# Writing the first five pairs of row gathers into the final stage of a hybrid decoder layer, the adding gather ahead of the plain one

## The chip, the cores and the metric

One core of a Trainium2 chip runs the whole kernel. The time is device microseconds of an execution. Five engines work beside each other: TensorE (PE, with its weight loads as PEld), VectorE (DVE), ScalarE (ACT), GpSimd (POOL) and SyncE (SP), and 16 DMA engines move data. Each engine takes its own instructions in order and waits for the others at semaphores. SP issues most plain transfers; POOL issues the indirect ones, and writes their descriptors itself.

## The reference, cut to what matters

The layer is a token mixer (attention and a gated delta rule), a layer norm, a mixture of experts and a last layer norm. The change touches the last two:

```python
h = layer_norm(DEEPNORM_ALPHA * h + mix, ln1_g[i], ln1_b[i])
ffn = hierarchical_moe(h.reshape(b * l, D_MODEL), ...)
h = layer_norm(DEEPNORM_ALPHA * h + ffn, ln2_g[i], ln2_b[i])
return h[:, N_META:]
```

In `hierarchical_moe` each of the 1024 tokens goes to one group of 4 and there to two experts of 8, so that of 32 experts two add a weighted row of 1024 numbers to the token. A token's last row is the layer norm of its own row plus these two expert rows.

## The kernel before, in words

The last phase (`phase4`) goes over the 32 experts in order. For each, POOL gathers the rows of up to 128 tokens from HBM (`gather`, line 1503), TensorE computes the expert, and POOL stores its 128 result rows to the HBM tensor `ysd` (`keep`, line 1576). Experts 30 and 31 are not stored: their rows stay in SBUF, and TensorE spreads them over the tokens with one-hot matrices `oh`. The loop over the experts runs under `manual_schedule`, in which every engine's instructions keep the order of the source; it ends with `self.man.close()` at line 1671.

For each of the eight token tiles t (128 tokens each) the final stage needs two gathers from `ysd`, made by `combine` (line 1579), 128 rows of 4 KB each:

- the **plain gather** writes one expert row per token into `ybs[t]`. These tiles lie in memory that held weights, so their names in the profile are `wo4l`, `wo6h`, `wo6l` and `wo4h`, two token tiles in each.
- the **adding gather** adds the other expert row, in the DMA engines, to `yts[t]` (`yt` in the profile), which holds the token's own row already.

`rows(t)` issues both. For t = 0 to 4 (`GE = 5`) it is called in `phase4` after `overflow`; for t = 5 to 7 it is called from the final stage.

`overflow` is a branch on a count `nov` that each engine loads and compares (lines 1693 and 1695). Its body handles tokens that an expert has no room for; here the count is zero and the body is jumped over, but the path around it is a block of its own, in which each engine waits at semaphores before it goes on. The adding gathers must come after the branch, because its body may add to `yts` too. The plain gathers need not, and outside `manual_schedule` a scheduler chooses the order.

`finish` is the final stage, again under `manual_schedule`. For a tile t, `total` lets TensorE sum the rows of experts 30 and 31 (line 1782: four matmuls in `part(t, 0)`, four in `part(t, 2)`) and the plain gather's tile through an identity matrix (line 1793) into PSUM; VectorE adds the sum to `yt` (line 1794). Then come `square` (ACT), `rstd` (DVE and POOL, lines 101 and 102), `shift` (DVE, line 1806), `scale` (ACT, line 120), `gain` (DVE, line 1812), `store` (DVE, line 1815, and the output's DMA from SP). `TO` gives each step a due time and the steps of all tiles are written out sorted by t + due time. `shift(t)` calls `more(t + GE)` first, so the pairs of gathers for tiles 5, 6 and 7 stand on POOL behind `rstd` of tiles 1, 2 and 3, and these stand behind `total` of tiles 2, 3 and 4 on VectorE.

Of the kernel before, what the change touches and what calls it, by code (L numbers as in the profile page):

```python
# [12 lines left out]
ALU = mybir.AluOpType  # L13
# [4 lines left out]
P = 128  # L18
# [9 lines left out]
NE = 32  # L28
# [19 lines left out]
GE = 5  # L48
# [33 lines left out]
class Trunk:  # L82
# [1394 lines left out]
    def phase4(self):  # L1477
# [100 lines left out]
        def combine(src, fi, n, t, k, o, **kw):  # L1578
            nc.gpsimd.indirect_dma_start(out=o, out_offset=None, in_=src,  # L1579
                                         in_offset=bass.IndirectOffsetOnAxis(ap=fi[:, t, k:k + 1], axis=0),  # L1580
                                         bounds_check=n - 1, oob_is_err=False, **kw)

        def rows(t):
            combine(self.ysd, fi, (NE - 2) * P + 1, t, 1, ybs[t])
            combine(self.ysd, fi, (NE - 2) * P, t, 0, yts[t], compute_op=ALU.add)

        def over(fi):
            for k in range(2):
# [19 lines left out]
        fi = self.small.tile([P, NT, 2], I32, name="fi", bufs=1)  # L1608
# [12 lines left out]
        for e in range(NE):  # L1621
            more = e + 1 < NE
# [23 lines left out]
            if e == FE:  # L1646
                self.rb.close()
                fp = fin.enter_context(self.pool("fin", "left"))
                yts = [fp.tile([P, D], F32, name=f"yt{t}") for t in range(NT)]
# [29 lines left out]
                                         in_=y, in_offset=None, bounds_check=16 * P - 1, oob_is_err=False)  # L1679

        self.overflow(item, ps, fp.tile([P, D], F32, name="xo"), over)
        for t in range(GE):
            rows(t)
        pss.close()
        sq = mp.tile([P, KT, P], F32R, name="xh", bufs=1).rearrange("p a b -> p (a b)")
        self.finish(fp, g2, b2, yts, oh, ys, sq, ybs, lambda t: t < NT and rows(t))
        fin.close()
        es.close()
# [81 lines left out]
    def finish(self, fp, g2, b2, yts, oh, ys, sq, ybs, more):  # L1770
        nc, tc = self.nc, self.tc
        st = [fp.tile([P, 4], F32, name=f"st{t}") for t in range(NT)]
        rs = [fp.tile([P, 2], F32, name=f"rs{t}") for t in range(NT)]
        with self.psum("psf") as ps, tc.manual_schedule():
            pfs = {}

            def part(t, j0):
                if j0 == 0:
                    pfs[t] = ps.tile([P, D], F32, name="pf", bufs=4)
                for c in range(2):  # L1780
                    for j in (j0, j0 + 1):
                        nc.tensor.matmul(pfs[t][:, c * 512:(c + 1) * 512], oh[j // 2][:, t],
                                         ys[j // 2][j % 2][:, c * 512:(c + 1) * 512], start=(j == 0), stop=False)

            part(0, 0)
            part(1, 0)
            def total(t):
                if t > 1:
                    part(t, 0)
                part(t, 2)  # L1790
                for c in range(2):
                    ns = slice(c * 512, (c + 1) * 512)
                    nc.tensor.matmul(pfs[t][:, ns], self.ident, ybs[t][:, ns], start=False, stop=True)
                nc.vector.scalar_tensor_tensor(yts[t], pfs.pop(t), 1.0, yts[t], op0=ALU.mult, op1=ALU.add,  # L1794
                                               accum_out=st[t][:, 0:1])

            def square(t):
                nc.scalar.activation(st[t][:, 1:2], st[t][:, 0:1], AF.Copy, scale=-1.0 / D)
                nc.scalar.activation(sq, yts[t], AF.Square, bias=st[t][:, 1:2], accum_out=st[t][:, 2:3])

            def rstd(t):
                self.rsqrt_into(rs[t][:, 0:1], st[t][:, 2:3], 1.0 / D, LN_EPS / ALPHA ** 2)

            def shift(t):
                more(t + GE)
                nc.vector.tensor_tensor(rs[t][:, 1:2], st[t][:, 1:2], rs[t][:, 0:1], op=ALU.mult)  # L1806

            def scale(t):
                self.ln_apply(yts[t], P, rs[t], yts[t])

            def gain(t):
                nc.vector.tensor_tensor(yts[t], yts[t], g2, op=ALU.mult)  # L1812

            def store(t):
                (nc.vector if t in TV else nc.gpsimd).tensor_tensor(yts[t], yts[t], b2, op=ALU.add)  # L1815
                nc.sync.dma_start(self.out[0, t * P:(t + 1) * P, :], yts[t])

            ops = (total, square, rstd, shift, scale, gain, store)
            for _, i, t in sorted((t + TO[i], i, t) for t in range(NT) for i in range(len(ops))):
                ops[i](t)  # L1820
# [59 lines left out]
```

## Time and profile before

| | us |
|---|---|
| median of 3 runs | 1189.67 (1184.7 to 1194.07) |
| profiled execution, its own time | 1192.47 |
| its span | 1190.7 |
| its mean granted TensorE clock | 0.953 |
| busy over the span: PE, DVE, ACT, POOL | 92%, 73%, 53%, 24% |

Starts are microseconds from the span's start. The change acts on the last 70 us alone: the end of the expert loop (to about 1126), the branch, and the final stage. The shares over the whole span say nothing on these, so the profile has to be read there by its timeline, its waits and its stretches.

### The profile page before, as it was taken

The page shows a single profiled execution, that of the slowest core. Times are in us where ns is not written, and L with a number is a line of the kernel's source. Part 1 is how long each engine was busy: PE and PEld are TensorE (multiplying, and loading weights), DVE is VectorE, ACT ScalarE, POOL GpSimd, SP SyncE. Part 2 cuts the span into 40 slices and gives each one's busy share as a digit, 9 for nine tenths or more (in the row PEclk, how much of TensorE's full clock was granted, in tenths as well). Part 3 has the DMA queues.
Part 4 walks back from the last instruction along what each step waited for, and adds up shares of the span by engine and source line. Part 5 has one row for each costly group of instructions (what it writes and reads, how often), then busy time and mean ns, then how long its engine had stood idle before and what let it go on. Part 6 is the DMA issues. An engine that isn't in the chain of part 4 may idle for free. (4 is left out here: it accounts for less than half of the span.)

```text
span 1190.7 us, 19809 instructions
## 1 busy us (share of the span) xinstructions
PE 1094.4 (92%) x7061; PEld 935.6 (79%) x7061; DVE 863.4 (73%) x1672; ACT 630.9 (53%) x1310; POOL 289.7 (24%) x389
## 2 busy tenths in 40 slices
PE   6999999999989979899989999857999999999973
PEld 4999999999989968777776777755777777777741
DVE  7941357988433238989847687786999999999827
ACT  3443346855223236566536464234777777777633
POOL 3523102412000013444324331001111111112253
PEclk9999999999999978999979999776999999999987
DMA  7411134466695577976547561756999999599676
GB/s 287 178 63 45 37 108 126 139 175 220 212 241 196 184 254 222 253 238 192 179 133 203 171 233 64 317 194 224 375 406 396 396 406 399 200 377 416 263 166 214
DMA packets 112441, 271.01 MB, mean 228 GB/s; under 512 B 31075, under 2 KB 60523, under 8 KB 99540
## 3 DMA queue, kind: packets, MB, share of 16 engines
q1 hardware_dynamic: 100816, 236.43, 57.6%
q0 software_dynamic: 11232, 32.22, 8.6%
q8 instruction: 57, 0.93, 0.3%
q10 hardware_dynamic: 292, 1.07, 0.2%
q14 instruction: 44, 0.36, 0.1%
HBM read 213.83 MB, written 64.53 MB: 234 GB/s over the span
## 5 line engine op out<-in xcount | busy, mean ns | idle before, releaser
L186 PE MATMUL pj<-hTh,wfh 128*128 128x346 f32 (+1 forms) x480 | 156.1, 325 | 0.1
L187 PE MATMUL pj<-hTl,wfh 128*128 128x346 f32 (+1 forms) x480 | 155.8, 325 | 0.0
L188 PE MATMUL pj<-hTh,wfl 128*128 128x346 f32 (+1 forms) x480 | 155.7, 324 | 0.0
L881 DVE TENSOR_TENSOR_SCAN mm<-mm,zero 128x272 f32<-128x272 f32 (+3 forms) x64 | 89.4, 1411 | 19.8 <-ACT mm L868 17.6
L186 PEld LDWEIGHTS pj<-hTh,wfh 128*128 128x128 f32 x480 | 90.8, 189 | 0.5 <-issue 0.3
L188 PEld LDWEIGHTS pj<-hTh,wfl 128*128 128x128 f32 x480 | 90.9, 189 | 0.1
L187 PEld LDWEIGHTS pj<-hTl,wfh 128*128 128x128 f32 x480 | 90.8, 189 | 0.2
L1535 PE MATMUL ph<-w13h,xh 128*128 128x512 f32 x192 | 88.6, 461 | 0.0
L179 PE MATMUL pj<-wvh,hTl 128*128 128x256 f32 (+3 forms) x280 | 78.9, 285 | 3.6 <-DVE hTl L97 3.5
L178 PE MATMUL pj<-wvl,hTh 128*128 128x256 f32 (+3 forms) x280 | 78.9, 284 | 2.2 <-DVE wvl L97 2.2
L177 PE MATMUL pj<-wvh,hTh 128*128 128x256 f32 (+3 forms) x280 | 79.5, 288 | 0.2 <-ACT hTh L96 0.2
L1465 DVE TENSOR_TENSOR w13l<-raw,w13h 128x512 fp32r<-128x512 f32 x126 | 77.9, 685 | 0.0
L1503 POOL DMA_INDIRECT xg<-h1d,ix x32 | 34.1, 1064 | 171.3 <-PE tp L1513 136.6
L1537 PE MATMUL ph<-w13h,xl 128*128 128x512 f32 x192 | 75.3, 392 | 0.0
L1536 PE MATMUL ph<-w13l,xh 128*128 128x512 f32 x192 | 74.9, 390 | 0.0
L1464 ACT ACTIVATE w13h<-raw 128x512 fp32r<-128x512 f32 x126 | 68.0, 621 | 0.0
L872 POOL TENSOR_SCALAR_AFFINE_SELECT mm<-mm 128x128 f32<-128x128 f32 x64 | 39.8, 627 | 111.9 <-ACT mm L868 111.5
L868 ACT ACTIVATE mm<-z 128x512 f32<-128x512 f32 (+1 forms) x80 | 44.3, 564 | 38.4 <-PE z L866 29.1
L866 PE MATMUL z<-qk 128*128 128x416 f32 (+6 forms) x224 | 59.8, 374 | 4.8 <-ACT kuw L778 2.9
L1465 DVE TENSOR_TENSOR w2l<-raw,w2h 128x512 fp32r<-128x512 f32 x96 | 59.9, 686 | 2.2 <-ACT w2h L1464 0.2
L96 ACT ACTIVATE xh<-tp 128x512 fp32r<-128x512 f32 x64 | 31.4, 491 | 50.1 <-DVE xf L1522 43.2
L902 ACT ACTIVATE wt<-tp 128x512 f32<-128x512 f32 (+1 forms) x80 | 41.6, 556 | 28.4 <-PE tp L901 27.7
(441 smaller groups left out, 2977.9 us busy)
## 6 DMA issues: line engine op xcount, KB each, us to landing
raw<-in_w SPq DMA_DIRECT2D x67, 1024.0 KB, 12.3
ysd<-y POOLq DMA_DIRECT2D x30, 512.0 KB, 8.5
qk<-qkd SPq DMA_DIRECT2D x16, 520.0 KB, 5.5
ht<-hscr SPq DMA_DIRECT2D x16, 512.0 KB, 3.4
wo4h<-in_w SPq DMA_DIRECT2D x8, 1024.0 KB, 13.4
wo4l<-in_w SPq DMA_DIRECT2D x7, 1024.0 KB, 14.0
wo6l<-in_w SPq DMA_DIRECT2D x7, 1024.0 KB, 12.1
wo6h<-in_w SPq DMA_DIRECT2D x7, 1024.0 KB, 11.4
```

What stands on the lines that cost most here:

```text
L177: nc.tensor.matmul(o[:p, :n], xh, wh[:, kt, ws], start=(kt == 0), stop=False)
L178: nc.tensor.matmul(o[:p, :n], xh, wl[:, kt, ws], start=False, stop=False)
L179: nc.tensor.matmul(o[:p, :n], xl, wh[:, kt, ws], start=False, stop=(kt == KT - 1))
L186: nc.tensor.matmul(o[:, :n], wh[:, kt], self.hTh[:, kt, c0:c0 + n], start=(kt == 0), stop=False)
L187: nc.tensor.matmul(o[:, :n], wh[:, kt], self.hTl[:, kt, c0:c0 + n], start=False, stop=False)
L188: nc.tensor.matmul(o[:, :n], wl[:, kt], self.hTh[:, kt, c0:c0 + n], start=False, stop=(kt == KT - 1))
L881: nc.vector.tensor_tensor_scan(mm[:, c0:c1][:, ::-1], mm[:, c0:c1][:, ::-1], self.zero1.to_broadcast([P, c1 - c0]), 1.0, op0=ALU.mult, op1 ...
L1464: nc.scalar.activation(wh, raw, AF.Copy)
L1465: (nc.gpsimd if k in pool else nc.vector).tensor_tensor(wl, raw, wh.bitcast(F32), op=ALU.subtract)
L1535: nc.tensor.matmul(ph, xh[:, kt], wh, start=False, stop=False)
L1536: nc.tensor.matmul(ph, xh[:, kt], wl, start=False, stop=False)
L1537: nc.tensor.matmul(ph, xl[:, kt], wh, start=False, stop=(kt == ks[-1]))
```

## The change

`rows(t)` issues the adding gather first and the plain one second; the loop that called it for t = 0 to 4 in `phase4` goes; and `finish` calls it for these five tiles as its first step, inside `manual_schedule`.

```diff
         def rows(t):
+            combine(self.ysd, fi, (NE - 2) * P, t, 0, yts[t], compute_op=ALU.add)
             combine(self.ysd, fi, (NE - 2) * P + 1, t, 1, ybs[t])
-            combine(self.ysd, fi, (NE - 2) * P, t, 0, yts[t], compute_op=ALU.add)
@@ phase4
         self.overflow(item, ps, fp.tile([P, D], F32, name="xo"), over)
-        for t in range(GE):
-            rows(t)
         pss.close()
@@ finish
         with self.psum("psf") as ps, tc.manual_schedule():
             pfs = {}
+            for t in range(GE):
+                more(t)
```

On POOL, at the end of the expert loop, the order before was this (`ysd<-y` are the expert stores, `wo..<-ysd` the plain gathers, and line 1695 is the branch over the overflow body):

```order
L1576 DMA ysd<-y 128x1024 x4
L1579 DMA wo4l<-ysd,fi 128x1024 x2
L1579 DMA wo6h<-ysd,fi 128x1024 x2
L1579 DMA wo6l<-ysd,fi 128x1024
L1693 TENSOR_LOAD nov
L1695 COMPARE_AND_BRANCH
```

The scheduler had put the five plain gathers ahead of the branch. In the changed kernel the branch follows the stores directly (its lines count two less):

```order
L1576 DMA ysd<-y 128x1024 x4
L1691 TENSOR_LOAD nov
L1693 COMPARE_AND_BRANCH
L1695 IOTA n_12659 128x16
```

The five plain gathers are gone from this place. The second place is POOL behind the branch's join, where the difference between the two kernels is this (`yt_` is the tile of an adding gather, and 11839 to 11843 are the token tiles 0 to 4):

```order
 L1579 DMA yt_11839<-ysd,fi 128x1024
+L1579 DMA wo4l<-ysd,fi 128x1024
 L1579 DMA yt_11840<-ysd,fi 128x1024
+L1579 DMA wo4l<-ysd,fi 128x1024
 L1579 DMA yt_11841<-ysd,fi 128x1024
+L1579 DMA wo6h<-ysd,fi 128x1024
 L1579 DMA yt_11842<-ysd,fi 128x1024
+L1579 DMA wo6h<-ysd,fi 128x1024
 L1579 DMA yt_11843<-ysd,fi 128x1024
```

The fifth plain gather (`wo6l`) follows right behind. Ten gathers now stand here where five stood, and each plain gather follows its tile's adding one. The third place is the wait of POOL on the path around the overflow body, which stands in both kernels with the same list (DMASW are the completion semaphores of the transfers that POOL issued):

```order
L1695 ISA [waits Pool_49,DMASW4_49,DMASW5_49,DMASW3_49,DMASW6_49,DMASW2_49,DMASW7_49,DMASW1_49,DMASW0_49]
```

It names every lane of POOL's transfers. What was issued on them last, ahead of it, is five plain gathers before and the expert stores now.

## Rows read from the trace of the kernel before

**Rows 1.** Chain of work that ended last, four of its pieces: start, us, what.

```profile
1128.27 10.39 DMA wo6h<-ysd,fi
1138.66 0.11 POOLq L1695
...
1173.53 1.23 DVE yt L1794 x2
...
1185.53 1.23 DVE yt L1815
```

**Rows 2.** Waits from 1118 us to the end: total us, times, longest.

```profile
DVE yt L1794 <- DMA yt<-ysd,fi: 25.3, 8, 13.8
```

**Rows 3.** Single lines 1695, 1579, 1576 (from 1090 us), 1503; durations ns min/median/max.

```profile
L1695 POOLq EVENT_SEMAPHORE  x5: 17/43/8036, 1125.7 to 1138.3; - x5
...
L1579 POOLq EVENT_SEMAPHORE  x15: 17/43/2768, 1118.5 to 1161.2; - x15
...
DMA to landing us min/median/max: 2.9/8.2/9.0
...
L1503 POOL DMA_INDIRECT xg<-h1d,ix x32: 986/1071/1316, 810.2 to 1085.7; - x32
```

**Rows 4.** Timeline of POOL: start, us, instruction, idle before it and its releaser.

```profile
1118.48 0.53 POOL L1576 DMA_DIRECT2D ysd<-y  x1 [9.13 <-ACT w2h L1464]
1122.46 4.17 POOL L1579 DMA_INDIRECT wo4l<-ysd,fi  x1 [3.45 <-issue]
...
1130.88 1.00 POOL L1579 DMA_INDIRECT wo6l<-ysd,fi  x1 [0.31 <-issue]
1139.73 1.61 POOL L1579 DMA_INDIRECT yt<-ysd,fi  x1 [7.86 <-issue]
...
1159.74 2.12 POOL L1579 DMA_INDIRECT yt<-ysd,fi  x1 [0.30 <-issue]
...
1162.65 1.05 POOL L1579 DMA_INDIRECT wo4h<-ysd,fi  x1 [0.18 <-issue]
```

**Rows 5.** Stretches: length, busy per engine, clock, DMA share (last but one), GB/s.

```profile
1121.00:1127.00 6.00, 5.30 (x24) 3.95 (x22) 5.45 (x9) 1.51 (x4) 4.23 (x2) 1.00 0.00 1
1127.40:1137.00 9.60, 7.33 (x24) 5.52 (x25) 3.34 (x5) 2.59 (x5) 3.56 (x4) 0.82 0.81 271
1137.00:1142.00 5.00, 5.00 (x16) 2.77 (x16) 0.00 (x0) 0.00 (x0) 1.97 (x2) 1.00 0.01 3
1142.00:1158.10 16.10, 12.15 (x43) 7.60 (x41) 5.28 (x14) 6.35 (x12) 10.19 (x9) 0.95 0.95 176
1158.10:1173.50 15.40, 11.42 (x28) 5.81 (x28) 10.89 (x18) 9.32 (x15) 9.49 (x8) 0.83 0.95 238
```

**Rows 6.** Timeline of DVE, the same columns.

```profile
1123.34 2.35 DVE L1637 TENSOR_TENSOR xg<-slots,ixt 128x1024 fp32r<-128x1024 f32 x2
...
1145.88 1.23 DVE L1794 SCALAR_TENSOR_TENSOR yt<-pf,yt 128x1024 f32<-128x1024 f32 x1 [13.81 <-DMA yt<-ysd,fi]
...
1158.08 1.23 DVE L1794 SCALAR_TENSOR_TENSOR yt<-pf,yt 128x1024 f32<-128x1024 f32 x1 [0.80 <-DMA yt<-ysd,fi]
...
1159.23 1.22 DVE L1812 TENSOR_TENSOR yt<-yt,g 128x1024 f32<-128x1024 f32 x1
...
1160.50 1.22 DVE L1815 TENSOR_TENSOR yt<-yt,b 128x1024 f32<-128x1024 f32 x1
1163.85 1.23 DVE L1794 SCALAR_TENSOR_TENSOR yt<-pf,yt 128x1024 f32<-128x1024 f32 x1 [2.14 <-DMA yt<-ysd,fi]
...
1169.10 1.23 DVE L1794 SCALAR_TENSOR_TENSOR yt<-pf,yt 128x1024 f32<-128x1024 f32 x1 [1.61 <-DMA yt<-ysd,fi]
```

**Rows 7.** Timeline of PE: the plain gather's tile through the identity matrix.

```profile
1137.05 1.88 PE L1793 MATMUL pf<-wo4l,ident 128*128 128x512 f32 x4
...
1150.44 1.88 PE L1793 MATMUL pf<-wo6l,ident 128*128 128x512 f32 x4
...
1159.43 3.78 PE L1793 MATMUL pf<-wo6l,ident 128*128 128x512 f32 x4 [5.28 <-DMA wo6l<-ysd,fi]
```

## The prediction

> **What bounds the kernel now.** I read the chain that ended last first, since only its end can move. Its last long piece is VectorE's adding of a tile's sum to `yt` for tile 7 at 1173.53; behind it stands VectorE work without a gap to 1186.76 and the last store to 1190.7 [rows 1]. So total(7), as I call that instruction, sets the end, and the 17.2 us behind it follow whenever it comes. Next I read the waits of this stage: VectorE waits for adding gathers 25.3 us in eight waits, the longest 13.8 us, which is the wait of total(0), at 1145.88 [rows 2, 6]. The final stage is therefore fed by POOL's gathers.
>
> Why does the first adding gather come so late? The chain answers: a plain gather landed at 1138.66, and only then POOL's queue left line 1695, the branch [rows 1]. The rows of that line show one wait of 8.0 us on POOL's queue [rows 3]. On the path around the overflow body POOL waits for all its transfers, and the last of these were the five plain gathers, issued from 1122.46 to 1131.88 [rows 4]. The stretches show the price: the DMA engines are idle from 1137 to 1142 (share 0.01), between the plain gathers (0.81) and the adding ones (0.95) [rows 5]. From 1142 they are nearly always busy, so that gap is most of what can be won.
>
> **The change, part by part.** Nothing is added or taken away: 16 gathers before, 16 after. Five plain ones move from ahead of the branch to behind it, each behind its adding one.
>
> *The join.* POOL's last transfer ahead of the branch is now the store at 1118.48 [rows 4]. It landed within 2.9 us (the shortest store; POOL's queue then waited at most 2.77 us for it ahead of the first gather) [rows 3]: 1121.4. From the landing at 1138.66 to the first adding gather at 1139.73 were 1.07 us [rows 1, 4]. So the first adding gather starts at 1122.5, not at 1139.73.
>
> *Its descriptors.* The gather that began at 1122.46 took 4.17 us, where the next ones took 1.00 [rows 4]. VectorE was then in operations with two SBUF inputs until 1125.69 [rows 6]; the gather ended 0.94 us behind that, about one gather's own time. The adding gather takes this place, and it needs 1.61 in place of 1.00 [rows 4]: I take 4.17 + 0.6 and end it at 1127.3. The bound from the other side is the 32 gathers of the expert loop at 1071 ns in the median, 1316 at most [rows 3], which means no block: then it ends at 1124.1, 3.2 us earlier. I take the blocked value, because that row has the same neighbours at the same time.
>
> *The DMA time.* The engines began to move data 0.7 us behind the end of the first adding gather (1141.34 to 1142.0) [rows 4, 5], so they begin at 1128.0 now, 14.0 us earlier. What they must move has grown, though: the plain gathers are in the same queue. A plain one costs 9.6 us x 0.81 / 5 = 1.55 us [rows 5]. An adding one costs (1158.08 - 1145.88) / 4 = 3.05 us [rows 6]; the first was added 3.9 us behind the start of the transfers, so a landing takes some 0.8 more. A pair is 4.6 us. Pairs 0 to 4: 1128.0 + 23.0 = 1151.0, landed at 1151.8. POOL writes a pair's descriptors in about 3.2 us (1.00 + 1.61 and two gaps of 0.3) [rows 4], less than 4.6, so the queue stays fed.
>
> *What is late next.* The plain tile now lands last, and behind it TensorE must take it through the identity matrix, 1.88 us [rows 7]. Before, this lay beside the wait for the adding gather (1137.05 against 1145.88); that cover is gone. TensorE reached tile 4's at 1150.44 [rows 7], so it now waits some 1.4 us there; for tiles 0 to 2 TensorE itself is the limit. total(4) comes at 1151.8 + 1.9 = 1153.7, before at 1158.08 [rows 6].
>
> *Pairs 5 to 7.* They stay behind rstd of tiles 1 to 3 on POOL, and so behind total(2) to total(4). The first gather of pair 7 followed total(4) by 4.57 us (1162.65 from 1158.08) [rows 4, 6]; now at 1158.3, with its descriptors 2.12 us (the dearest adding one) [rows 4] and 0.7 to the transfers: 1161.1. Pairs with one output store beside them cost 5.25 and 4.43 us, by total(5) to total(7) at 1163.85, 1169.10 and 1173.53 [rows 1, 6], on average 4.84. Pairs 5 and 6 end at 1151.0 + 9.7 = 1160.7; pair 7 starts at 1161.1 and ends at 1165.9. With 0.8 for landing and 1.9 for TensorE, total(7) comes at 1168.6 in place of 1173.53: **4.9 us earlier**.
>
> *The skill's rule.* The Trainium skill ("SBUF — State Buffer", section "SBUF: two separate sides") says that VectorE and GpSimd share a port pair under an exclusive lock, so that GpSimd cannot write descriptors until such a VectorE operation ends. The row at 1122.46 agrees with that. The row at 1159.74 does so only in part: VectorE's lines 1812 and 1815 covered it until 1161.72, yet it ended at 1161.86 after 2.12 us [rows 4, 6]; a full lock would have left its 1.6 us to be done behind 1161.72. By the full lock, the adding gather of pair 7 could be pushed behind two such operations (2 x 1.22 us), and the gain would be 4.9 - 2.4 = 2.5 us.
>
> *Bounds of the pair's price.* With 4.43 for all eight, transfers end at 1163.4 and the gain is 7.4; with 5.25 they end at 1170.0 and it is 0.8. No row shows adding and plain gathers alternate without stores.
>
> Sum: the span goes from 1190.7 to 1185.8, the profiled execution from 1192.47 to 1187.6. That execution lies 2.8 us above the median of the runs; against the median of 1189.67 the forecast is **1184.8 us**.
>
> **The rivals.**
> - *The branch still holds POOL* (slower). If something else than the plain gathers keeps POOL at the join to 1138, all eight pairs start at 1142.0 and total(7) comes at 1168.6 + 14.0 = 1182.6, 9.1 us later: 1198.8. It decides from a first adding gather later than 1127.4, where the 4.9 us are used up. For it: the wait names every lane, also POOL's own. Against it: the chain has a plain gather's landing right ahead of its end [rows 1], and the store needs 2.9 us only [rows 3]. Chance 0.07.
> - *No block on the first gather.* Transfers begin at 1124.8, gain 8.1, time 1181.6. For it: the 32 gathers at 1071 ns, many beside a busy VectorE. Against it: the 4.17 us row. Chance 0.2.
> - *Alternating gathers cost more*, 5.25 us a pair, and TensorE, waiting between tiles, falls to its lower clock, at which the identity takes 3.78 us as at 1159.43 [rows 7]: -0.8 + 1.9 = 1.1 us slower, 1190.8; with one of the two, 1186.7 to 1188.9. For it: TensorE's 5.28 us wait there was followed by that clock. Against it: the expected waits are about 1.2 us a tile (4.6 less 3.35 of matmuls, a quarter of the way from 1137.05 to 1150.44) [rows 7]. Chance 0.18.
> - *The late gathers wait for VectorE.* The adding gather of pair 7 begins behind both operations of lines 1812 and 1815, 2.4 us later: gain 2.5, 1187.2. For it: it stands beside them, as the one at 1159.74 did. Against it: that one took 2.12 us only [rows 4]. Chance 0.05.
>
> **How the numbers follow.** The forecast (gain 3 to 6.5) has 0.5. The predicted time is its 1184.8, for which the range takes in the gain without the block (1181.6) less 3 us, and the dear pairs with the lower clock (1190.8) plus 2: three runs of the kernel before spread over 9.4 us, and their median can be off by some 3. That is 1178.5 to 1193. Left out are the first rival and a gain beyond 11 us. About 1%, 11.9 us, is what a measurement of this kernel can tell from no change. Faster than that needs the unblocked gather and cheap pairs together (8.1 + 2.5 = 10.6) and more: 0.05. Slower needs the first rival with dear pairs (9.1 + up to 4.1): 0.04. Within 1%: 0.91.
>
> **What would show it.** Right: the wait of 8.0 us on line 1695's POOL queue shrinks to under 3; the first `yt` gather starts near 1122.5 and takes over 4 us; the idle 5 us of the DMA engines are gone; total(0) comes near 1139, total(4) near 1153.7, total(7) near 1168.6; the identity of tiles 3 to 7 waits for `wo` gathers; 17.2 us remain behind total(7). Wrong: a first `yt` gather behind 1127.4; pairs beyond 5.3 us; the identity of the late tiles at 3.8 us; or DMA idle between pairs 6 and 7.

## The result, and the profile after

The changed kernel takes 1184.26 us in the median of 20 runs (1180.01 to 1191.7), the kernel before 1190.36 in 20 (1184.37 to 1194.38). The ratio is 0.995 (95% interval 0.9933 to 0.9967), which is 4 to 8 us less. The forecast was 1184.8. In a later comparison beside other experiments the same kernel gave 0.9964 (0.9928 to 0.9999).

The profiled execution of the changed kernel has a span of 1178.9 us, 11.8 less than that of before. That is not the gain. POOL's last expert store begins at 1118.48 in the one and at 1111.55 in the other, so 6.9 us of it lie ahead of the first instruction that the change moves, where both kernels do the same. From here on I count from that store, in each trace. Behind it the span is 72.2 us before and 67.4 now, **4.9 us** less, and the forecast was 4.9.

POOL's timeline of the changed kernel answers to [rows 4] (start, us, instruction, idle before it):

```profile
1111.55 0.53 POOL L1576 DMA_DIRECT2D ysd<-y  x1 [9.13 <-ACT w2h L1464]
1116.84 3.46 POOL L1579 DMA_INDIRECT yt<-ysd,fi  x1 [4.76 <-issue]
1120.61 1.05 POOL L1579 DMA_INDIRECT wo4l<-ysd,fi  x1 [0.30 <-issue]
...
1140.98 1.60 POOL L1579 DMA_INDIRECT yt<-ysd,fi  x1 [0.22 <-issue]
...
1150.24 1.60 POOL L1579 DMA_INDIRECT yt<-ysd,fi  x1 [0.19 <-issue]
```

The first adding gather starts 5.3 us behind the store; it was 21.25. The branch's line has lost its long wait, as the row that answers to the first of [rows 3] shows (durations in ns, then the first and the last start):

```profile
L1693 POOLq EVENT_SEMAPHORE  x5: 17/43/43, 1112.6 to 1114.9; - x5
```

The stretches answer to [rows 5] (the last two columns are the DMA share and GB/s):

```profile
1114.50:1120.50 6.00, 4.91 (x22) 3.58 (x20) 5.01 (x8) 1.44 (x5) 3.46 (x1) 1.00 0.00 0
1120.50:1141.20 20.70, 17.74 (x58) 11.84 (x59) 7.23 (x14) 6.52 (x13) 12.71 (x12) 0.92 0.98 241
1141.20:1144.00 2.80, 2.80 (x11) 1.86 (x10) 1.36 (x4) 1.82 (x5) 2.47 (x3) 1.00 0.48 82
1144.00:1161.70 17.70, 14.85 (x41) 7.76 (x40) 10.91 (x18) 10.00 (x15) 10.35 (x8) 0.90 0.83 232
1161.70:1178.90 17.20, 0.01 (x1) 0.00 (x0) 13.15 (x17) 5.06 (x6) 3.05 (x2) 0.65 0.43 174
```

The idle 5 us between the two groups of transfers are gone: ten gathers move in one run of 20.7 us. A new, smaller hole has opened behind them (share 0.48). The 17.2 us behind tile 7 are unchanged. VectorE's addings answer to [rows 6]:

```profile
1132.59 1.23 DVE L1794 SCALAR_TENSOR_TENSOR yt<-pf,yt 128x1024 f32<-128x1024 f32 x1 [7.46 <-PE pf L1793]
...
1145.98 1.22 DVE L1794 SCALAR_TENSOR_TENSOR yt<-pf,yt 128x1024 f32<-128x1024 f32 x1 [2.23 <-PE pf L1793]
...
1153.23 1.23 DVE L1794 SCALAR_TENSOR_TENSOR yt<-pf,yt 128x1024 f32<-128x1024 f32 x1 [3.61 <-PE pf L1793]
...
1161.74 1.23 DVE L1794 SCALAR_TENSOR_TENSOR yt<-pf,yt 128x1024 f32<-128x1024 f32 x1 [1.23 <-PE pf L1793]
```

Seven of the eight wait for TensorE now, where all eight waited for adding gathers [rows 2]. TensorE's identity matmuls of tiles 5, 6 and 7 answer to [rows 7]:

```profile
1149.61 3.58 PE L1793 MATMUL pf<-wo6l,ident 128*128 128x512 f32 x4 [1.84 <-DMA wo6l<-ysd,fi]
1154.96 1.88 PE L1793 MATMUL pf<-wo4h,ident 128*128 128x512 f32 x4
1159.72 1.98 PE L1793 MATMUL pf<-wo4h,ident 128*128 128x512 f32 x4 [1.01 <-DMA wo4h<-ysd,fi]
```

Tile 5's plain gather comes late, and its matmuls take 3.58 us in place of 1.88, at a granted clock of 0.55 (the column ahead of the DMA share; 0.50 is TensorE's lower level of 1.2 GHz, 1.00 the upper of 2.4):

```profile
1149.60:1152.20 2.60, 2.59 (x4) 1.04 (x5) 0.02 (x1) 0.26 (x1) 2.10 (x3) 0.55 0.92 252
```

### The profile page after: what moved, and what is told of

It reads as the page before. It is cut to its first block, busy times and chain, and to the rows that moved or that the text cites. A ratio compares the mean times of both kernels' runs of the same rounds, so it can differ in the third digit from the quotient of the medians.

```text
span 1178.9 us, 19811 instructions
## 1 busy us (share of the span) xinstructions
PE 1091.0 (93%) x7061; PEld 932.1 (79%) x7061; DVE 862.4 (73%) x1672; ACT 630.9 (54%) x1310; POOL 289.6 (25%) x389
## 3 DMA queue, kind: packets, MB, share of 16 engines
q10 hardware_dynamic: 292, 1.07, 0.2%
```

## The experiments

Each row below is worked out from one trace: the start of the instruction less the start of that trace's last expert store, in us. T0, T4 and T7 are VectorE's addings of tiles 0, 4 and 7. The ratio is to the kernel before, with its interval.

| kernel | first adding gather | T0 | T4 | T7 | ratio |
|---|---|---|---|---|---|
| before | 21.25 | 27.40 | 39.60 | 55.05 | 1 |
| changed | 5.29 | 21.04 | 34.43 | 50.19 | 0.995 (0.9933 to 0.9967) |
| changed, again | 5.30 | 19.48 | 34.11 | 49.28 | 0.9964 (0.9928 to 0.9999) |
| order only | 21.15 | 27.66 | 38.35 | 55.20 | 0.9996 (0.9969 to 1.0023) |
| place only | 13.57 | 19.86 | 36.61 | 50.97 | 0.9965 (0.9935 to 0.9994) |
| eight pairs ahead | 5.28 | 19.84 | 34.43 | 46.20 | 0.9925 (0.9894 to 0.9955) |
| six pairs ahead | 5.27 | 19.54 | 33.47 | 45.30 | 0.9925 (0.9897 to 0.9952) |
| one-hot later | 5.29 | 20.50 | 33.84 | 49.23 | 0.9957 (0.9924 to 0.999) |
| eight ahead, one-hot later | 5.28 | 21.96 | 35.32 | 46.07 | 0.9907 (0.9867 to 0.9948) |
| six ahead, one-hot later | 5.27 | 20.43 | 33.77 | 44.47 | 0.9933 (0.9905 to 0.9961) |
| adding ones first, then plain ones | 5.29 | 29.98 | 43.62 | 59.36 | one run only |

My theory was that the gain comes from POOL leaving the branch early, since no plain gather is under way there. Its rivals: the order in the pair does it, or the fuller DMA queue by itself.

**Order only.** The pair is swapped, the loop stays in `phase4`.

```diff
         def rows(t):
+            combine(self.ysd, fi, (NE - 2) * P, t, 0, yts[t], compute_op=ALU.add)
             combine(self.ysd, fi, (NE - 2) * P + 1, t, 1, ybs[t])
-            combine(self.ysd, fi, (NE - 2) * P, t, 0, yts[t], compute_op=ALU.add)
```

> Only the order in the pair is changed (adding gather first); the five pairs stay ahead of the branch in the source. The scheduler still puts the five plain gathers ahead of the branch, so POOL has the same order there as before; only pairs 5 to 7 have the adding one first. Theory (the gain comes from POOL leaving the branch early, because no plain gather is under way): the wait on line 1695's POOL queue stays near 8 us, the first adding gather stays 21 us behind the last expert store (5.3 us in the changed kernel), and the adding of tile 7 stays 55 us behind that store or comes 1 to 2 us later, since the plain tile's identity matmuls now follow the last landing: 0 to +2 us. Rival (the order in the pair gives the gain): 3 to 6 us faster than before.

T7 at 55.20 and a ratio of 0.9996, and the long wait at the branch is still there (8.05 us): the order in the pair alone gives nothing that can be measured. The rival falls.

```profile
L1695 POOLq EVENT_SEMAPHORE  x5: 17/42/8052, 1118.7 to 1131.1; - x5
```

**Place only.** The loop is in the final stage, with the plain gather first.

```diff
         with self.psum("psf") as ps, tc.manual_schedule():
             pfs = {}
+            for t in range(GE):
+                more(t)
...
         self.overflow(item, ps, fp.tile([P, D], F32, name="xo"), over)
-        for t in range(GE):
-            rows(t)
```

> Only the place is changed: the five pairs are written into the final stage, but with the plain gather first. One plain gather (tile 0) is then still put ahead of the branch, the other four stand behind it. Theory: the join waits for that one gather, so the wait on the POOL queue at the branch is 4 to 7 us, and the first adding gather comes 12 to 14 us behind the last expert store (before 21.3, changed kernel 5.3). The adding of tile 7 comes 50 to 53 us behind the store (before 55.1, changed 50.2): 2 to 5 us faster than before. Rival (the join does not wait for gathers under way): first adding gather 6 to 8 us behind the store.

One plain gather is still put ahead of the branch, and it shows what such a gather costs. POOL's queue at the branch, and POOL's timeline:

```profile
L1693 POOLq EVENT_SEMAPHORE  x5: 17/43/43, 1124.3 to 1131.2; - x5
```

```profile
1119.50 0.53 POOL L1576 DMA_DIRECT2D ysd<-y  x1 [9.13 <-ACT w2h L1464]
1123.49 4.17 POOL L1579 DMA_INDIRECT wo4l<-ysd,fi  x1 [3.45 <-DVE w13l L1465]
1133.07 1.63 POOL L1579 DMA_INDIRECT yt<-ysd,fi  x1 [5.41 <-issue]
```

The five semaphore instructions take from 1124.3 to 1131.2 in place of 2.3 us, and the first adding gather comes at 13.57. With five, one and no plain gather ahead of the branch it comes at 21.25, 13.57 and 5.29: the join waits for what is under way, as the theory has it. T7 at 50.97 is as expected. So most of the gain is the place: 4.1 us of the 4.9 in these traces. That the adding gather stands first keeps the last plain gather from being hoisted, and wins 8.3 us at the first adding gather, yet only 0.8 at T7 in these two traces, less than the two traces of the changed kernel differ by (0.9); the ratios can't tell the two kernels apart. Here the DMA engines are full from 1135.5 us to nearly the last landing, without the hole of the changed kernel:

```profile
1135.50:1169.50 34.00, 29.19 (x90) 17.36 (x88) 16.17 (x31) 15.78 (x26) 23.46 (x20) 0.95 1.01 255
```

So a later start without a hole comes out almost level with an earlier start with one. The other rival, the fuller queue by itself, is not parted from the early exit: moving the loop brings both, and no run has a full queue behind the old, late exit. The last experiment below shows only that an early exit together with a full queue is not enough.

**Eight pairs ahead.** `GE = 5` becomes `GE = 8` in the changed kernel.

```diff
-GE = 5
+GE = 8
```

> The changed kernel with GE = 8: all eight pairs are issued at the start of the final stage, none waits behind rstd. In the changed kernel the DMA engines ran half empty 30 to 33 us behind the last store (share 0.59 and 0.52) because pair 5 waits for total(2). Theory: that hole and the wait of TensorE for the plain gather of tile 5 (1.8 us, then the lower clock) go; pairs at about 4.0 us put the adding of tile 7 at 45 to 47 us behind the last store (changed 50.2), 3 to 5 us faster than the changed kernel, 8 to 10 us faster than before. Rival 1 (pairs cost 4.6 us, the queue is the bound): 49 to 50 us, no gain over the changed kernel. Rival 2: rstd on POOL, now behind all gathers, delays the normalisation, so that more than 17.2 us remain behind tile 7's adding.

T7 comes at 46.20, and the DMA engines work from the first transfer to near the last without a hole (stretch of this kernel):

```profile
1127.50:1158.00 30.50, 26.48 (x91) 16.47 (x91) 13.32 (x26) 12.74 (x23) 21.72 (x19) 1.00 1.02 261
```

The second rival's wait is there too: rstd stands on POOL behind 16 gathers, and VectorE waits for it in its own order, here ahead of tile 3's adding:

```profile
1150.96 0.16 DVE L1806 TENSOR_TENSOR rs<-st,rs 128x1 f32<-128x1 f32 x1 [5.56 <-POOL rs L102]
```

No cost of it shows at the end: TensorE goes on through tiles 3 and 4 meanwhile, T4 is at 34.43 as in the changed kernel, and 17.2 us remain behind T7.

**Six pairs ahead.** `GE = 6`.

> The changed kernel with GE = 6: pair 5 is issued with the first five, pairs 6 and 7 behind rstd of tiles 1 and 2. Theory (the hole in the DMA queue before pair 5 costs the changed kernel some 4 us): one pair ahead is enough to fill it, so no stretch behind the start of the transfers has a DMA share under 0.8, TensorE does not fall to its lower clock at tile 5, and the adding of tile 7 comes 46 to 47.5 us behind the last store (changed kernel 50.2, all eight ahead 46.2), without the wait of VectorE for rstd that eight ahead brought (5.6 us). Rival (what counted with eight ahead was only that TensorE happened to start at its full clock, 1.2 us): 48.5 to 50 us.

T7 comes at 45.30, a little under the range expected. VectorE has no wait for rstd in this trace, and one pair ahead is enough to close the hole (a stretch, then T7):

```profile
1119.00:1148.00 29.00, 25.68 (x89) 16.14 (x88) 12.71 (x24) 12.61 (x22) 21.84 (x19) 1.00 1.04 259
...
1154.78 1.23 DVE L1794 SCALAR_TENSOR_TENSOR yt<-pf,yt 128x1024 f32<-128x1024 f32 x1 [0.45 <-PE pf L1793]
```

The clock is 1.00 throughout here, and the profile of the changed kernel taken beside it also started TensorE at the full clock (T0 at 19.48) and still had T7 at 49.28. It kept that clock at tile 5 too, where its matmuls took 1.98 us:

```profile
1156.73 1.98 PE L1793 MATMUL pf<-wo6l,ident 128*128 128x512 f32 x4 [1.99 <-DMA wo6l<-ysd,fi]
```

So neither the clock at the start nor the one at tile 5 makes the 4 us; the rival falls. Twelve us around the hole, first in the changed kernel's first trace, then in its second:

```profile
1139.55:1151.55 12.00, 10.16 (x32) 5.99 (x31) 5.64 (x14) 7.73 (x12) 9.22 (x8) 0.93 0.77 180
1146.81:1158.81 12.00, 10.01 (x34) 5.90 (x33) 5.39 (x15) 7.73 (x12) 9.49 (x8) 1.00 0.81 189
```

The DMA engines lose 2.8 and 2.3 us there, which six ahead do not lose. That idle time is more than half of the 4 to 5 us; where the rest goes is not shown.

**One-hot later.** VectorE's two one-hot operations move behind the last transpose's copies.

```diff
                 self.split_k(self.raws_of(e), range(KT, 12), pcs[e], (), True)
-                for i in (1, 0):
-                    nc.vector.tensor_tensor(oh[i], ...)
                 sg = swiglu(ph)
                 yo = down(act, pcs.pop(e - 1))
                 act = apose(sg)
+                for i in (1, 0):
+                    nc.vector.tensor_tensor(oh[i], ...)
```

> The changed kernel with VectorE's two one-hot operations (line 1637, two SBUF inputs, 2.35 us together) moved behind the last swiglu and the copies of its transpose. Theory (the first gather's descriptors wait for such VectorE work): the first adding gather takes 1.6 to 2.2 us instead of 3.46 and the transfers begin 1.3 to 1.9 us earlier behind the last store. Tiles 0 to 4 are bound by TensorE there, so the time gains less: 0 to 2 us against the changed kernel. Rival (a first gather behind a pause costs some 3.5 to 4 us by itself): it still takes 3.4 us or more.

The first adding gather takes 1.68 us, not 3.46; the second, which the moved operations now cover, takes 2.48, not 1.56. POOL's rows, then VectorE's (line 1640 is the moved one):

```profile
1119.12 1.68 POOL L1579 DMA_INDIRECT yt<-ysd,fi  x1 [4.76 <-issue]
...
1122.46 2.48 POOL L1579 DMA_INDIRECT yt<-ysd,fi  x1 [0.30 <-issue]
```

```profile
1122.30 2.35 DVE L1640 TENSOR_TENSOR xg<-slots,ixt 128x1024 fp32r<-128x1024 f32 x2
```

The delay moves with the VectorE work: it is no price of a first gather. T7 gains 1.0 against the one trace of the changed kernel and 0.05 against the other, and the ratio is in the same interval: not measurable.

**Both together**, with eight and with six ahead.

> All eight pairs ahead (GE = 8) and VectorE's one-hot operations moved behind the copies of the last transpose, together. Theory (independent terms): 4.0 and 1.0 us against the changed kernel add up, the adding of tile 7 comes 45 to 46 us behind the last store, 9 to 10 us less than before, about 0.8% of the time. Rival (TensorE is the bound with eight ahead, and its start does not move): 46 to 47 us, nothing added.

T7 at 46.07 lies just outside the expected 45 to 46 and inside the rival's 46 to 47. But TensorE fell to its lower clock 1.0 us into the stage in this execution (0.51 from 1135.20 to 1138.55, T0 at 21.96), so this is undecided.

> The version the experiments point to: six pairs ahead (GE = 6) and VectorE's one-hot operations moved behind the copies of the last transpose. Theory: no hole in the DMA queue, no long wait of VectorE for rstd, the first adding gather unblocked (1.7 us): the adding of tile 7 comes 44.5 to 46 us behind the last store, 9 to 10.5 us less than before, 0.991 to 0.993 of its time, and not to be told from six pairs ahead alone (45.3 us). Rival (the unblocked gather does add its 1 us): 44.3 us or less.

T7 at 44.47 is the lowest, at the edge of the expected 44.5 to 46. From T1 at 23.07 on it is 3.57 us a tile in this trace, six times: TensorE is the bound to the end. The ratio, 0.9933, can't be told from that of six ahead alone (0.9925). Both are faster than before. Against the changed kernel beside it (0.9928 to 0.9999) the interval of six ahead (0.9897 to 0.9952) still overlaps, so that they are better than the change rests on the traces, which show some 4 us.

**Adding gathers first, then the plain ones**, in the changed kernel (the part of the edit in `finish`; `rows` takes the choice of gather as an argument).

```diff
+            for k in range(2):
                 for t in range(GE):
-                    more(t)
+                    more(t, (k,))
```

> The changed kernel, but the five adding gathers are issued first and the five plain ones behind them, instead of in turns. Theory (a gather costs the queue its own time, 1.6 us plain and 2.7 adding, whatever stands beside it; some 4.0 us a pair in turns): the ten transfers take 20 to 21.5 us as in turns (20 us), but the first plain tile lands only some 16 to 17 us behind the first transfer, so the adding of tile 0 comes 27 to 29 us behind the last store (changed 21.0), tiles 0 to 4 then follow at TensorE's pace of 3.6 us, and tile 7 comes 53 to 56 us behind it. Rival (turns cost extra, as the prediction's third rival had it): the ten transfers take 18 us or less.

Stretches of this trace: the adding gathers alone, the plain ones alone, and what follows.

```profile
1129.00:1139.00 10.00, 4.71 (x20) 3.25 (x18) 2.11 (x3) 1.38 (x2) 7.99 (x7) 0.99 1.03 188
1142.00:1146.00 4.00, 1.22 (x2) 0.70 (x3) 0.00 (x0) 0.00 (x0) 0.00 (x0) 0.50 1.02 410
1148.00:1158.00 10.00, 10.00 (x32) 6.12 (x31) 3.90 (x9) 4.50 (x10) 1.81 (x3) 0.95 0.03 9
```

The engines are full in both, at 188 and 410 GB/s; at these rates 512 KB take 2.8 and 1.3 us, 4.1 a pair. The ten transfers end some 20 us behind their start, as in turns: turns cost nothing. T0 at 29.98 and T7 at 59.36 are later than I expected (27 to 29, 53 to 56). For T0, TensorE's matmuls of tile 0 ran at the lower clock (0.50 in the second stretch):

```profile
1144.78 3.78 PE L1796 MATMUL pf<-wo4l,ident 128*128 128x512 f32 x4 [8.25 <-DMA wo4l<-ysd,fi]
```

The last stretch says why for T7: with T2 so late, pair 5 leaves the DMA engines idle for ten microseconds. This is the hole of the changed kernel in large. POOL leaves the branch as early here as in the changed kernel, and T7 is still later than in the kernel before: behind an early exit the order counts, since a tile is done only when both its gathers have landed.

## Why the prediction was right, point by point

- *The join* was right: the first adding gather leaves when the store has landed. It came at 5.3 behind the store, 1.3 later than forecast: the store landed 3.2 us behind its issue in place of 2.9 (the row), and from that landing to the gather were 2.1 us, where I had carried over 1.07. Why it is 2.1 is open.

```profile
DMA to landing us min/median/max: 3.2/3.2/3.2
```

- *Its descriptors* were right in their end. The gather took 3.46, not 4.8 (4.17 + 0.6), because it began later beside the same VectorE work; it ended 8.75 us behind the store, forecast 8.8. That the wait is for VectorE was argued then and is shown now by the one-hot later.
- *The DMA time* was mis-sized, and nothing else in this part: a pair costs 20.7 x 0.98 / 5 = 4.1 us, not 4.6. The 3.05 us of the adding gather were read from VectorE's addings, over a stretch at whose end the queue was running dry; 2.8 is what full engines show. The plain one's 1.55 was too high as well: full engines show 1.3, and why the five plain gathers of the kernel before took longer is open. The third rival's first half, that turns cost more, is out.
- *What is late next.* Tile 4 was to wait for its plain gather; with the cheaper pair TensorE is the limit through tile 4 instead, and T4 came at 34.4, forecast 35.2.
- *Pairs 5 to 7: the step that failed.* I worked out the issue of pair 7 and took it that pair 5 finds the queue still fed. It does not: its adding gather starts at 29.4, behind rstd of tile 1 and so behind T2 at 27.3, and the cheaper pairs have emptied the queue by then. The hole (2.8 us at a share of 0.48) made tile 5's plain gather late; TensorE idled from 1147.8 to 1149.6 and did its identity matmuls at the lower clock (0.55), 3.58 us in place of 1.88, which is the second half of the third rival, at one tile. T5 came at 41.7, where the forecast's steps give 40.0; in the second trace, without the lower clock, it came at 39.95. Six pairs ahead closes this hole, and T7 moves by 4 to 5 us.
- *Sum.* The pairs' price was too high by 0.5 us each, and the hole was left out; the two cancel, so T7 at 50.19 (forecast 50.1) is right by mechanism and partly by luck in size. That the traces differ by just the 4.9 us forecast is luck too: with the second trace of the changed kernel (T7 at 49.28) they differ by 5.8, and the medians by 6.1. The identity behind the last landing is there as forecast: 1.98 us at 1159.72, then VectorE.
- *The cheap bound* was worked out wrongly: the gain of 7.4 with 4.43 us a pair leaves out that pair 7 moves only when POOL has issued it. By the prediction's own steps that bound is 6.2.
- *Two of the signs* did not come: the first adding gather took less than 4 us, and of tiles 3 to 7 only 5 and 7 waited for their plain gather on TensorE.
- *The late gathers wait for VectorE*: pairs 5 to 7 have 1.59 to 1.60 us for each adding gather, so this rival did not happen, but it was hardly tried either: no gather of these three stood beside lines 1812 and 1815. It was POOL's rstd ahead of pair 7 that stood beside line 1815 and took 1.54 us in place of some 0.57:

```profile
1148.40 1.22 DVE L1815 TENSOR_TENSOR yt<-yt,b 128x1024 f32<-128x1024 f32 x1
1148.50 1.54 POOL L102 TENSOR_TENSOR rs<-rs,mhalf 128x1 f32<-128x1 f32 x1 [0.89 <-DVE rs L1806]
```

- *The skill's rule.* VectorE's one-hot work, with two SBUF inputs, ran until 1118.75 in the changed kernel, and the first adding gather ended 1.55 us behind it, a whole gather's time. In the one-hot experiment the gather at 1122.46 ended 0.3 us behind that work, not a whole gather. The Trainium skill's lock ("SBUF — State Buffer", section "SBUF: two separate sides") fully blocks the later of the two; for a VectorE operation with two SBUF inputs the page says so only against a GpSimd operation that reads SBUF. The first of these gathers agrees with a full block, the second does not: the delay goes where such VectorE work goes, but it is not always a full block.

```profile
1116.40 2.35 DVE L1637 TENSOR_TENSOR xg<-slots,ixt 128x1024 fp32r<-128x1024 f32 x2
```

## What to carry to other kernels

A branch that is not taken can still be a barrier: here the path around it waited for every transfer that POOL had under way, so hoisting five harmless gathers ahead of it held back five that mattered. Before moving transfers up, look for the join that waits for them. And when a queue is filled in two helpings, check that the second is issued before the first has drained, by the faster of the prices that the rows allow.

## What the runs showed of the hardware that was not expected

The adding gather moved 188 GB/s with the DMA engines full, the plain one 410, and in turns they neither helped nor hindered each other (4.1 us a pair either way). TensorE started the final stage at 0.50 of its clock in some executions and at 1.00 in others of the same kernel, as in the two traces of the changed kernel:

```profile
1126.50:1129.20 2.70, 2.70 (x6) 2.13 (x7) 0.00 (x0) 0.00 (x0) 2.09 (x3) 0.50 0.94 203
1133.50:1136.38 2.88, 2.83 (x13) 2.37 (x14) 0.00 (x0) 0.00 (x0) 2.27 (x3) 1.00 0.98 226
```

T0 differs by 1.6 us between them (21.04 and 19.48), which no edit made; at T4 0.3 us of it is left. At tile 5 the same two traces part again: TensorE was idle for 1.8 us and then ran at 0.55 in the first, idle for 2.0 us and then ran at 1.00 in the second.
